# Attention softmax: context scores copied out of PSUM by VectorE with scale and minimum, one maximum per head, small two-input work moved to GpSimd

## The chip, the cores and the metric

The kernel runs on one core of a Trainium2 chip. A core has five engines with a queue each: TensorE (matmul; PE in the profile, its weight loads PEld), VectorE (DVE), ScalarE (ACT), GpSimd (POOL) and SyncE (SP, which issues DMAs here). An engine takes its instructions in the order of its queue, so an instruction that waits holds up all behind it. TensorE's results land in PSUM, which VectorE and ScalarE read; everything else lies in SBUF. The metric is device time in microseconds of one execution; the smaller the better.

## The reference

One layer of a diffusion backbone over 1024 latent tokens of width 1024, with 256 context tokens. After a modulated projection there are two attention branches with 8 query heads and 2 kv heads each (so 4 query heads to a kv head), head size 64:

```
A (windowed): scores of 128 queries against their block, the one before and the one after
              (band |q - k| <= 128), and the 256 context keys;
              m = max(scores, sink);  e = exp(scores - m);  p = e / (sum(e) + exp(sink - m))
B (global):   q and k normalised (RMS); scores against all 1024 latent and 256 context keys;
              p = softmax(scores)
o = p @ v     in each branch
y = (sigmoid(g_a) * (o_a @ w_a) + sigmoid(g_b) * (o_b @ w_b)) @ w_out
x = LN(alpha * x + gate * y), then a convolutional SwiGLU and a second LN
```

In both branches latent and context keys share one softmax. Everything is float32.

## The kernel before

The projections come first (to about 345 us of the profile), then attention, the merge with the branch matrices and `w_out`, and the feed-forward part from there to the end. float32 products are made of three or two products of float32r pieces: a tensor is split into a high part (a cast) and a low part (the difference).

Attention works in 32 units, `Unit(br, i, g)`: branch, block of 128 queries, kv group. The 16 units of branch A come first, then the 16 of B. A unit has two halves. The score half does, per head `h`, `lat(h)`: matmuls into a PSUM tile `s` (two buffers of 128x1024), a VectorE instruction which copies the scores out to `p`, multiplied by the negated scale, with the running minimum written to `nm` (so `nm` is minus the maximum), and ScalarE's `soft`, the exponential with its row sum in `sm`. `norm` then makes the reciprocal of the sum. The value half (`value_steps`) comes one unit later: `tr_step` transposes 128 keys of all four heads on TensorE into a PSUM tile (three buffers), ScalarE casts the high part `pth`, VectorE makes the low part `ptl` (for a few steps ScalarE copies out `prw` and GpSimd makes both); `av_step` multiplies them with the values into `av`; `out_step` copies `av` out as `avs`, adds its two halves (high and low part of the values) into `ot`, multiplies by the reciprocal sums `rb` and splits into `O`. `up` moves the second half to the first 64 partitions for that addition. `rows` turns the reciprocals `sm` into rows (a transposition `str`, a copy, a DMA to DRAM and two DMAs back that spread them over the partitions) for `rb`.

Branch A takes the scores of window and context together: a head's 640 columns (512 at the edges) are one `p` tile, and `norm` adds the exponential of the sink. Branch B has 1024 latent columns a head; its 256 context columns of all four heads stand in one tile, made ahead of the latent ones by `cxp`, and normalised by a maximum of their own: `reduce_max` (L470), a product with the scale (L471), and four exponentials straight from PSUM. The latent copies start from that maximum (`self.other`, `scalar2` of L458), so `nm` covers both, and `norm` brings the context side to it: a factor `f` (L482, L483), four products on GpSimd over the context probabilities (L486), and two small operations that join the sums (L487, L488). In branch A, `f` is the sink's term (L490 to L492).

The Python loop at L832 interleaves the two halves of consecutive units and, from unit 18 on, steps of the first branch matrix (`b`, `bT`, its weights split by GpSimd as `hwb`, `lwb`). The order in which the instructions finally stand on each engine is set by the build's scheduler, from priorities and its own estimate of times; so a small change of the source can move instructions of its neighbours too. GpSimd's queue also carries DMA issues (`sd`, L600) and the split of the queries (`qs`, in `qprep`, two units ahead).

Of the kernel before, what the change touches and what calls it, by code (L numbers as in the profile page):

```python
# [10 lines left out]
ALU = mybir.AluOpType  # L11
# [10 lines left out]
FF = 2816  # L22
NF = FF // P
GRID = 64
LN_EPS = 1e-5
QK_EPS = 1e-6
ALPHA = 2.0 ** 0.25
# [39 lines left out]
def layer_kernel(  # L67
# [315 lines left out]
    class Unit:  # L383
# [43 lines left out]
        def lat(self, h):  # L427
            kh = self.br * 2 + self.g
            s = None if self.w == 256 and h in S1 else s_tile(f"s{self.id}_{h}")
            if s is None:  # L430
                s = pt_tile(f"s{self.id}_{h}")
                self.qk(s[:, 0:256], h, KL[kh][:, self.k0:self.k0 + 256], False)
                if self.i == 0:
                    nc.tensor.matmul(s[:, 128:256], identr, maskr[:, 1], start=False, stop=True)
                else:
                    nc.tensor.matmul(s[:, 0:128], identr, maskr[:, 0], start=False, stop=True)
                self.qk(s[:, 256:512], h, KC[0][:, kh])
                o = s
            elif self.br == 1:
                for c in (0, 512):  # L440
                    self.qk(s[:, c:c + 512], h, KL[kh][:, c:c + 512])
                o = s
            else:
                w = self.w
                l = s[:, 512 - w:512]
                self.qk(l, h, KL[kh][:, self.k0:self.k0 + w], False)
                if w == 384:
                    nc.tensor.matmul(l.rearrange("p (a b) -> p a b", b=P)[:, 0::2, :], identr, maskr,
                                     start=False, stop=True)
                elif self.i == 0:  # L450
                    nc.tensor.matmul(l[:, 128:256], identr, maskr[:, 1], start=False, stop=True)
                else:
                    nc.tensor.matmul(l[:, 0:128], identr, maskr[:, 0], start=False, stop=True)
                self.qk(s[:, 512:512 + NC], h, KC[0][:, kh])
                o = s[:, 512 - w:512 + NC]
            hs = slice(h, h + 1)
            p = p_tile(f"p{self.id}_{h}")[:, 0:T if self.br else self.w + NC]
            nc.vector.tensor_scalar(out=p, in0=o, scalar1=self.qscale(nqs)[:, hs] if self.br else -1.0,  # L458
                                    scalar2=self.other[:, hs], op0=ALU.mult, op1=ALU.min, accum_out=self.nm[:, hs])
            self.soft(p, p, h, self.nm, self.sm, -1.0)  # L460
            self.pc[h, 0] = p

        def cxp(self):
            kh = self.br * 2 + self.g
            s = s_tile(f"s{self.id}_x")
            for h in range(4):
                self.qk(s[:, h * NC:(h + 1) * NC], h, KC[0][:, kh])
            self.other = small(f"nmc_{self.id}", (P, 4))
            self.smc = small(f"smc_{self.id}", (P, 4))
            nc.vector.reduce_max(self.other, s.rearrange("p (a b) -> p a b", a=4), axis=AX.X)  # L470
            nc.vector.tensor_tensor(out=self.other, in0=self.other, in1=self.qscale(nqs), op=ALU.mult)  # L471
            p = p_tile(f"p{self.id}_x")
            for h in range(4):
                self.pc[h, 1] = p[:, h * NC:(h + 1) * NC]
                self.soft(s[:, h * NC:(h + 1) * NC], self.pc[h, 1], h, self.other, self.smc,
                          self.qscale(pqs)[:, h:h + 1])

        def norm(self):
            hc = slice(self.g * 4, self.g * 4 + 4)
            f = small(f"f_{self.id}", (P, 4))  # L480
            if self.br:
                nc.vector.tensor_tensor(out=f, in0=self.nm, in1=self.other, op=ALU.subtract)  # L482
                nc.scalar.activation(f, f, AF.Exp)  # L483
                for h in range(4):
                    p = self.pc[h, 1]
                    nc.gpsimd.tensor_scalar(out=p, in0=p, scalar1=f[:, h:h + 1], scalar2=0.0, op0=ALU.mult, op1=ALU.add)  # L486
                nc.vector.tensor_tensor(out=self.smc, in0=self.smc, in1=f, op=ALU.mult)  # L487
                nc.vector.tensor_tensor(out=self.sm, in0=self.sm, in1=self.smc, op=ALU.add)  # L488
            else:
                nc.vector.tensor_tensor(out=f, in0=self.nm, in1=sinkb[:, hc], op=ALU.add)  # L490
                nc.scalar.activation(f, f, AF.Exp)
                nc.vector.tensor_tensor(out=self.sm, in0=self.sm, in1=f, op=ALU.add)  # L492
            nc.vector.reciprocal(self.sm, self.sm)

        def rows(self):
# [26 lines left out]
        def value_steps(self):  # L522
            nm, kt = self.id, self.kt
            vh = self.br * 2 + self.g
            parts = {}

            def tr_step(n):
                tr = pt_tile(f"ptr{nm}_{n}")
                for h in range(4):
                    nc.tensor.transpose(tr[:, h * P:(h + 1) * P], self.pslice(h, n), ident)  # L530
                hi = att.tile([P, 512], R32, tag="pth", name=f"pth{nm}_{n}", bufs=4)
                lo = att.tile([P, 512], R32, tag="ptl", name=f"ptl{nm}_{n}", bufs=4)
                pooled = n in POOL_LO[self.br]
                if pooled:
                    rw = att.tile([P, 512], F32, tag="ptr", name=f"prw{nm}_{n}", bufs=2)
                    nc.scalar.copy(rw, tr)  # L536
                    split(rw, hi, lo, nc.gpsimd, nc.gpsimd)
                else:
                    nc.scalar.copy(hi, tr)  # L539
                    nc.vector.tensor_tensor(out=lo, in0=tr, in1=hi.bitcast(F32), op=ALU.subtract)  # L540
                parts[n] = hi, lo
                return pooled

            def av_step(n):
                first = self.left == len(kt)
                self.left -= 1
                if first:
                    self.av = ps2.tile([P, 512], F32, tag="av", name=f"av{nm}")
                hi, lo = parts.pop(n)
                v = VT[kt[n] // 2][:, kt[n] % 2, vh]  # L550
                nc.tensor.matmul(self.av, v, hi, start=first, stop=False)  # L551
                nc.tensor.matmul(self.av, v, lo, start=False, stop=self.left == 0)  # L552

            def out_step():
                av = self.av
                avs = att.tile([P, 512], F32, tag="ptr", name=f"avs{nm}", bufs=2)
                nc.scalar.copy(avs, av)  # L557
                up = att.tile([HD, 512], F32, tag="up", name=f"up{nm}", bufs=1)
                nc.gpsimd.tensor_scalar(out=up, in0=avs[HD:P], scalar1=1.0, scalar2=0.0, op0=ALU.mult, op1=ALU.add)
                ot = att.tile([P, 2, P], F32, tag="ot", name=f"ot{nm}", bufs=1)  # L560
                for h in range(2):
                    nc.vector.tensor_tensor(out=ot[h * HD:(h + 1) * HD],
                                            in0=avs[0:HD].rearrange("p (a b q) -> p a b q", b=2, q=P)[:, :, h],
                                            in1=up.rearrange("p (a b q) -> p a b q", b=2, q=P)[:, :, h], op=ALU.add)
                nc.gpsimd.tensor_tensor(out=ot, in0=ot, in1=self.rb, op=ALU.mult)
                hf = self.i // 4
                qs = slice((self.i % 4) * P, (self.i % 4 + 1) * P)
                split(ot, otile(self.br, hf, 0, self.g)[:, :, qs], otile(self.br, hf, 1, self.g)[:, :, qs],
                      nc.gpsimd, nc.gpsimd)

            def step(ns):
                pooled = [tr_step(n) for n in ns]
                for n, pl in zip(ns, pooled):
                    clk[0] += 1
                    avq.append((self, n, clk[0] + LAG[self.br] + (PLAG[self.br] if pl else 0)))
                    av_issue()

            self.left = len(kt)
            self.av_step, self.out_step = av_step, out_step
            g = 1 + self.br  # L580
            steps = [lambda n=n: step(range(n, n + g)) for n in range(0, len(kt), g)]
            steps.insert(2 - self.br, self.rows)
            return steps

    tokens = []
# [184 lines left out]
    def small(name, shape):  # L770
        return att.tile(list(shape), F32, tag=name.split("_")[0], name=name,
                        bufs=4)
# [977 lines left out]
```

## Time and profile before

| what | value |
|---|---|
| time, median of 3 runs | 1577.16 us (1576.5 to 1577.59) |
| the profiled execution | 1580.51 us, span 1578.6 us, TensorE clock 0.994 |
| busy: PE, PEld, DVE, ACT, POOL | 1528.4, 1264.6, 1198.0, 808.9, 756.5 us |
| reciprocals of branch A (first, last) | 353.29, 475.50 us |
| reciprocals of branch B (first, last) | 489.43, 763.38 us |

A row of a timeline has the start and the length in us, engine, line, operation, output<-inputs, shapes, a count, and in brackets the idle time of the engine just before it and what ended it. When several equal instructions are merged, the length is that of all. A group has the count, the busy time, the mean of one in ns, and the idle time before them with what ended it. A stretch has its length, then busy time and count of PE, PEld, DVE, ACT and POOL, the clock, the DMA share and the DMA rate. A line of waits has the waiting instruction, the one waited for, us in total, times, and the longest. Line numbers are those of the kernel before, unless a row is of another kernel.

### The profile page before, as it was taken

How to read it: one execution, taken by the hardware profiler on the slowest of the kernel's cores; microseconds unless marked ns; L12 is line 12 of the kernel's file. 1: busy time of each engine (PE TensorE's matmuls, PEld its weight loads, DVE VectorE, ACT ScalarE, POOL GpSimd, SP SyncE). 2: the span in 40 equal slices, each digit the busy share in tenths (PEclk: the TensorE clock that was granted, in tenths of full speed). 3: DMA queues.
4: the chain of work that ended last, by engine and by line, in shares of the span. 5: the costliest groups of instructions: out<-in, count | busy, mean ns of one | idle time of the engine just before them, and what ended most of it. 6: DMA issues, size and time to landing. Idle time of an engine off the chain costs nothing.

```text
span 1578.6 us, 21930 instructions
## 1 busy us (share of the span) xinstructions
PE 1528.4 (97%) x7614; PEld 1264.6 (80%) x7614; DVE 1198.0 (76%) x1761; ACT 808.9 (51%) x1439; POOL 756.5 (48%) x737
## 2 busy tenths in 40 slices
PE   6999999999999999999999999999999999999997
PEld 5878788878886887777788898888888888888886
DVE  7797645628888777788675679888888888656797
ACT  5422222448888667688522466444444444435533
POOL 0573312426666566655432544666667765021053
PEclk9999999999999999999999999999999999999999
DMA  9685662322227555532344132333334446996723
GB/s 378 218 313 187 213 219 87 120 79 74 64 82 180 138 128 127 128 84 41 130 160 93 54 107 81 121 107 107 107 107 107 107 111 178 364 270 221 244 92 107
DMA packets 112015, 230.25 MB, mean 146 GB/s; under 512 B 13504, under 2 KB 27328, under 8 KB 111808
## 3 DMA queue, kind: packets, MB, share of 16 engines
q1 hardware_dynamic: 96464, 199.20, 37.9%
q0 software_dynamic: 10400, 20.19, 8.2%
q10 hardware_dynamic: 5040, 9.46, 1.6%
q8 instruction: 60, 0.98, 0.3%
q14 instruction: 51, 0.42, 0.1%
HBM read 177.61 MB, written 65.87 MB: 154 GB/s over the span
## 4 chain that ended last, share of the span: by engine, by line
PE 73%; DVE 12%; DMA 5%; ACT 4%; issue 3%; POOL 1%; SPq 0%; ACTq 0%; DVEq 0%; POOLq 0%
PE ptr L530 5%; PE b L91 3%; PE b L90 3%; PE b L89 3%; PE g L89 3%; PE g L91 3%; PE g L90 3%; PE s L413 2%; PE av L551 2%; PE c L90 2%; PE d L90 2%; PE a L90 2%; PE c L89 2%; PE d L89 2%; PE a L89 2%
## 5 line engine op out<-in xcount | busy, mean ns | idle before, releaser
L540 DVE TENSOR_TENSOR ptl<-ptr,pth 128x512 fp32r<-128x512 f32 x188 | 124.6, 684 | 27.8 <-ACT pth L539 25.6
L86 DVE TENSOR_TENSOR ld<-rd,hd 128x1024 fp32r<-128x1024 f32 x77 | 97.6, 1284 | 50.8 <-ACT hd L81 48.7
L530 PE MATMUL ptr<-ident,p 128*128 128x128 f32 x816 | 126.7, 278 | 9.2 <-DVE ptl L540 6.8
L539 ACT CAST pth<-ptr 128x512 fp32r<-128x512 f32 x188 | 106.5, 588 | 56.5 <-PE ptr L530 32.8
L425 ACT ACTIVATE p<-p,nm 128x1024 f32<-128x1024 f32 (+2 forms) x128 | 125.3, 981 | 11.1 <-DVE p L458 10.3
L530 PEld LDWEIGHTS ptr<-ident,p 128*128 128x128 f32 x816 | 93.6, 140 | 39.6 <-DVE ptl L540 13.9
L81 ACT CAST hd<-rd 128x1024 fp32r<-128x1024 f32 x77 | 79.4, 1050 | 88.5 <-PE p L91 60.4
L551 PE MATMUL av<-pth,VT 128*128 128x512 f32 x236 | 104.6, 443 | 1.0 <-ACT avs L557 0.5
L90 PE MATMUL p<-ld,hd 128*128 128x512 f32 x264 | 103.5, 392 | 0.3 <-DVE ld L86 0.3
L89 PE MATMUL p<-hd 128*128 128x512 f32 x264 | 103.8, 393 | 0.0
L91 PE MATMUL p<-hd,ld 128*128 128x512 f32 x264 | 103.5, 392 | 0.0
L89 PE MATMUL g<-hh,whg 128*128 128x512 f32 x256 | 99.9, 390 | 0.0
L91 PE MATMUL g<-hh,wlg 128*128 128x512 f32 x256 | 99.7, 389 | 0.0
L90 PE MATMUL g<-hl,whg 128*128 128x512 f32 x256 | 99.6, 389 | 0.0
L552 PE MATMUL av<-ptl,VT 128*128 128x512 f32 x236 | 97.7, 414 | 1.9 <-POOL ptl L86 1.8
L86 POOL TENSOR_TENSOR wlg<-wg,whg 128x512 fp32r<-128x512 f32 x32 | 44.2, 1388 | 112.7 <-ACT whg L81 109.2
L458 DVE TENSOR_SCALAR_CACHE_REDUCE p<-s,cvt,nmc 128x1024 f32<-128x1024 f32 x64 | 84.4, 1339 | 12.3 <-PE s L414 11.8
L413 PE MATMUL s<-KL,q 128*128 128x512 f32 (+2 forms) x192 | 76.0, 396 | 2.9 <-ACT p_x L425 2.0
L187 DVE CUSTOM_DVE_ANT_0 wml<-wml,sc,bmc 128x1024 f32<-128x1024 f32 x32 | 45.6, 1435 | 40.6 <-DMA wml<-in_wmodT_dram 39.7
L83 POOL TENSOR_SCALAR pth<-prw 128x512 fp32r<-128x512 f32 x48 | 31.0, 646 | 87.8 <-ACT prw L536 62.3
L414 PE MATMUL s<-KL,q 128*128 128x512 f32 (+2 forms) x192 | 71.7, 373 | 0.0
L81 ACT CAST wS<-s 128x512 fp32r<-128x512 f32 x76 | 45.3, 621 | 51.0 <-POOL s L1083 50.2
(402 smaller groups left out, 4945.7 us busy)
## 6 DMA issues: line engine op xcount, KB each, us to landing
wml<-in_wmodT_dram SPq DMA_DIRECT2D x48, 512.0 KB
ru<-in_w_up_dram SPq DMA_DIRECT2D x38, 512.0 KB
rd<-td SPq DMA_DIRECT2D x55, 256.0 KB
rd<-sd SPq DMA_DIRECT2D x44, 256.0 KB
rd<-in_w_dn_dram SPq DMA_DIRECT2D x33, 256.0 KB
wm<-in_wmodT_dram SPq DMA_DIRECT2D x16, 512.0 KB
wg<-in_w_g_dram SPq DMA_DIRECT2D x32, 256.0 KB
sgd<-sg ACTq DMA_DIRECT2D x32, 256.0 KB
```

Source lines behind the costliest of these rows:

```text
L81: cast[:] = [nc.scalar.copy(hi, src).ins]
L86: low[:] = [lo_eng.tensor_tensor(out=lo, in0=src, in1=hi.bitcast(F32), op=ALU.subtract).ins]
L89: nc.tensor.matmul(ps, a[0], b[0], start=start, stop=False, skip_group_check=resumed)
L90: nc.tensor.matmul(ps, a[0], b[1], start=False, stop=False, skip_group_check=resumed)
L91: nc.tensor.matmul(ps, a[1], b[0], start=False, stop=stop, skip_group_check=resumed)
L413: nc.tensor.matmul(o, self.q[0][:, hs], ks, start=True, stop=False)
L425: nc.scalar.activation(p, s, AF.Exp, bias=nm[:, h:h + 1], scale=scale, accum_out=sm[:, h:h + 1])
L530: nc.tensor.transpose(tr[:, h * P:(h + 1) * P], self.pslice(h, n), ident)
L539: nc.scalar.copy(hi, tr)
L540: nc.vector.tensor_tensor(out=lo, in0=tr, in1=hi.bitcast(F32), op=ALU.subtract)
L551: nc.tensor.matmul(self.av, v, hi, start=first, stop=False)
L552: nc.tensor.matmul(self.av, v, lo, start=False, stop=self.left == 0)
```

## The change

In branch B `cxp` no longer takes a maximum of the context scores. For each head it copies the 256 context scores out of PSUM to `p`, scaled and negated, with their minimum written to `other`; the latent copy starts from it as before. The exponentials of the context columns come after those of the latent ones of the same head, from SBUF and with the head's one maximum `nm`, so that the factor `f`, the four products on GpSimd and the joining of unequal sums go away; what is left is one addition of two sums. Small additions with two SBUF inputs (`sm` of both branches, `f` of branch A, and the two halves of `ot`) are issued on GpSimd in place of VectorE. `rows` stands one step later among the value steps: in branch A after three transposition steps in place of two, in B after the second pair in place of the first.

```diff
+TOP = 3.0e38
...
             self.soft(p, p, h, self.nm, self.sm, -1.0)
             self.pc[h, 0] = p
+            if self.br:
+                self.soft(self.pc[h, 1], self.pc[h, 1], h, self.nm, self.smc, -1.0)
 
         def cxp(self):
...
-            nc.vector.reduce_max(self.other, s.rearrange("p (a b) -> p a b", a=4), axis=AX.X)
-            nc.vector.tensor_tensor(out=self.other, in0=self.other, in1=self.qscale(nqs), op=ALU.mult)
             p = p_tile(f"p{self.id}_x")
             for h in range(4):
-                self.pc[h, 1] = p[:, h * NC:(h + 1) * NC]
-                self.soft(s[:, h * NC:(h + 1) * NC], self.pc[h, 1], h, self.other, self.smc,
-                          self.qscale(pqs)[:, h:h + 1])
+                c = slice(h * NC, (h + 1) * NC)
+                self.pc[h, 1] = p[:, c]
+                nc.vector.tensor_scalar(out=p[:, c], in0=s[:, c], scalar1=self.qscale(nqs)[:, h:h + 1], scalar2=TOP,
+                                        op0=ALU.mult, op1=ALU.min, accum_out=self.other[:, h:h + 1])
 
         def norm(self):
             hc = slice(self.g * 4, self.g * 4 + 4)
-            f = small(f"f_{self.id}", (P, 4))
-            if self.br:
-                nc.vector.tensor_tensor(out=f, in0=self.nm, in1=self.other, op=ALU.subtract)
-                nc.scalar.activation(f, f, AF.Exp)
-                for h in range(4):
-                    p = self.pc[h, 1]
-                    nc.gpsimd.tensor_scalar(out=p, in0=p, scalar1=f[:, h:h + 1], scalar2=0.0, op0=ALU.mult, op1=ALU.add)
-                nc.vector.tensor_tensor(out=self.smc, in0=self.smc, in1=f, op=ALU.mult)
-                nc.vector.tensor_tensor(out=self.sm, in0=self.sm, in1=self.smc, op=ALU.add)
-            else:
-                nc.vector.tensor_tensor(out=f, in0=self.nm, in1=sinkb[:, hc], op=ALU.add)
-                nc.scalar.activation(f, f, AF.Exp)
-                nc.vector.tensor_tensor(out=self.sm, in0=self.sm, in1=f, op=ALU.add)
+            more = self.smc if self.br else small(f"f_{self.id}", (P, 4))
+            if not self.br:
+                nc.gpsimd.tensor_tensor(out=more, in0=self.nm, in1=sinkb[:, hc], op=ALU.add)
+                nc.scalar.activation(more, more, AF.Exp)
+            nc.gpsimd.tensor_tensor(out=self.sm, in0=self.sm, in1=more, op=ALU.add)
             nc.vector.reciprocal(self.sm, self.sm)
...
                 for h in range(2):
-                    nc.vector.tensor_tensor(out=ot[h * HD:(h + 1) * HD],
+                    nc.gpsimd.tensor_tensor(out=ot[h * HD:(h + 1) * HD],
                                             in0=avs[0:HD].rearrange("p (a b q) -> p a b q", b=2, q=P)[:, :, h],
                                             in1=up.rearrange("p (a b q) -> p a b q", b=2, q=P)[:, :, h], op=ALU.add)
...
             steps = [lambda n=n: step(range(n, n + g)) for n in range(0, len(kt), g)]
-            steps.insert(2 - self.br, self.rows)
+            steps.insert(3 - self.br, self.rows)
             return steps
```

## The prediction

> **What bounds the kernel now.** I read the page's engine totals first, then busy time by stretch for the two attention stages, and then the timeline of single engines inside one unit of branch A. A unit is one (branch, query block, kv group); A is the windowed branch (`br` 0), B the global one (`br` 1).
>
> ```profile
> PE 1528.4 (97%) x7614; PEld 1264.6 (80%) x7614; DVE 1198.0 (76%) x1761; ACT 808.9 (51%) x1439; POOL 756.5 (48%) x737
> 383.40:458.90 75.50, 75.14 (x497) 63.64 (x496) 65.47 (x154) 64.79 (x154) 48.93 (x73) 1.00 0.25 67
> 505.80:763.40 257.60, 248.33 (x1415) 201.59 (x1415) 202.83 (x350) 188.23 (x417) 149.88 (x206) 1.00 0.45 104
> ```
>
> TensorE looks full (its ends are modelled), so idle time has to be looked for in the order of the queues. The two stretches run from the first to the last of ten reciprocals of A, and over nearly all of B. In A VectorE (third figure) and ScalarE (fourth) are at 87% and 86%, GpSimd at 65%; in B VectorE is at 79%.
>
> ```profile
> 383.41 0.18 DVE L493 RECIPROCAL sm<-sm 128x4 f32<-128x4 f32 x1
> 458.88 0.18 DVE L493 RECIPROCAL sm<-sm 128x4 f32<-128x4 f32 x1
> ...
> 424.68 0.48 DVE L492 TENSOR_TENSOR sm<-sm,f 128x4 f32<-128x4 f32 x1 [1.02 <-ACT f L491]
> 425.19 0.18 DVE L493 RECIPROCAL sm<-sm 128x4 f32<-128x4 f32 x1
> 425.28 0.85 DVE L458 TENSOR_SCALAR_CACHE_REDUCE p<-s,negsink 128x640 f32<-128x640 f32 x1
> 426.06 1.88 DVE L540 TENSOR_TENSOR ptl<-ptr,pth 128x512 fp32r<-128x512 f32 x3
> 427.86 0.87 DVE L458 TENSOR_SCALAR_CACHE_REDUCE p<-s,negsink 128x640 f32<-128x640 f32 x1
> 428.66 0.88 DVE L458 TENSOR_SCALAR_CACHE_REDUCE p<-s,negsink 128x640 f32<-128x640 f32 x1
> 431.17 0.93 DVE L562 TENSOR_TENSOR ot<-avs,up 64x256 f32<-64x256 f32 x2
> 432.13 0.16 DVE L490 TENSOR_TENSOR f<-nm,sinkb 128x4 f32<-128x4 f32 x1
> ```
>
> One reciprocal ends each unit. From 383.41 to 458.88 there are nine steps: 75.47 / 9 = 8.39 us per unit. In the unit shown VectorE runs nearly without a gap; its one steady wait is 1.02 us before `sm`, for ScalarE's exponential of the sink. So VectorE's queue closes the loop in A. Two starts in a row give the pitch of an instruction: a score copy 0.80, a `ptl` 0.60 (1.80 for three), a reciprocal 0.09.
>
> **The change in stage A.** VectorE loses two `ot` additions, `f` and `sm`. The additions go to GpSimd's queue, and what matters is where they stand. In the built program GpSimd's order for one inner A unit (here 0_3_0 to 0_3_1) is:
>
> ```
> sm 3_0 | qs 5_0 (cast) | up 2_1 | qs 5_0 (low part) | ot 2_1 x2 | ot*rb 2_1 | O cast | O low | f 3_1 | pth 3_0 | ptl 3_0 | sm 3_1
> VectorE: reciprocal 3_0 | ptl | ptl | score copy 3_1, head 0 | ptl | copy | copy | ptl | copy | reciprocal 3_1 ...
> ScalarE: f 3_0 | pth x4 | exp 3_1, head 0 | avs 2_1 | exp | exp | rb | q | prw | exp | f 3_1 ...
> ```
>
> VectorE's reciprocal now waits for GpSimd's `sm`; behind it in VectorE's queue stand the next unit's `ptl` and score copies, for which TensorE, and through ScalarE's first exponential `avs`, wait; and GpSimd's `up` waits for that `avs`. This is a closed loop through three engines, and all of GpSimd's output work lies on it. Its prices:
>
> ```profile
> 423.82 0.62 POOL L83 TENSOR_SCALAR pth<-prw 128x512 fp32r<-128x512 f32 x1 [1.06 <-DMA rb<-dn]
> 424.40 0.73 POOL L565 TENSOR_TENSOR ot<-ot,rb 128x256 f32<-128x256 f32 x1
> 425.10 1.28 POOL L86 TENSOR_TENSOR ptl<-prw,pth 128x512 fp32r<-128x512 f32 x1
> 426.35 0.40 POOL L83 TENSOR_SCALAR O<-ot 128x256 fp32r<-128x256 f32 x1
> 426.83 0.73 POOL L86 TENSOR_TENSOR O<-ot,O 128x256 fp32r<-128x256 f32 x1
> 429.46 0.41 POOL L83 TENSOR_SCALAR qs<-Q 128x256 fp32r<-128x256 f32 x1 [1.90 <-PE qtr L403]
> 429.95 0.61 POOL L559 TENSOR_SCALAR up<-avs 64x512 f32<-64x512 f32 x1
> 430.65 0.74 POOL L86 TENSOR_TENSOR qs<-Q,qs 128x256 fp32r<-128x256 f32 x1
> ...
> 429.19 0.59 ACT L557 COPY avs<-av 128x512 f32<-128x512 f32 x1
> 429.66 0.84 ACT L425 ACTIVATE p<-p,nm 128x640 f32<-128x640 f32 x1
> 430.49 0.83 ACT L425 ACTIVATE p<-p,nm 128x640 f32<-128x640 f32 x1
> ...
> 429.37 0.42 PE L413 MATMUL s<-KL,q 128*128 128x384 f32 x1
> 430.04 0.28 PE L414 MATMUL s<-KC,q 128*128 128x256 f32 x1
> ...
> L321 POOL TENSOR_SCALAR cvt<-cvt 128x8 f32<-128x8 f32 x8 | 2.5, 307 | 0.7
> ```
>
> From one reciprocal to the next:
> - Reciprocal to the end of the next head-0 copy: 0.09 + 2 x 0.60 + 0.80 = 2.1 us. Then either exponential and `avs` on ScalarE (pitch 0.83, copy 0.59: 3.5 us), or, in every second unit, where `av`'s last product is queued on TensorE behind a score group waiting for that copy's buffer, 0.8 us of the group, its product and the copy, some 3.9. `qs` before `up` waits for a transposition behind the same group, to about 4.0. I take 3.9 to the start of `up`. In the trace `up` starts 4.76 us after the reciprocal (425.19 to 429.95), with one `ptl` more ahead of it, so 3.9 is no pessimism.
> - `up` 0.70, `qs` 0.74, two `ot`, `ot*rb` 0.73, `O` 0.48 and 0.74. The 64x256 addition is not in the trace on GpSimd; a 64x512 `up` costs what a 128x512 `pth` does, so its price goes by the free size: the 128x256 addition at 0.73 is nearest. Bounds: 0.40 (the one-input `O` cast) and 0.93 (VectorE's pair as one). With 1.46 for two the piece is 4.85.
> - `f`, `pth` 0.58, `ptl` 1.25, `sm`. Of a 128x4 addition on GpSimd the nearest row is 128x8 with one input, 0.31; bounds 0.16 (VectorE's `f`) and 0.40. 2.45, and 0.1 for hand-overs.
>
> Sum 3.9 + 4.85 + 2.45 + 0.1 = 11.3 us against 8.39, so +2.9 on nine inner steps: +26 us. With both low prices the loop is 10.3 (+17), with both high ones 11.9 (+31). GpSimd's pitches alone add up to some 8.0, so it is not full: it stands idle in front of `avs`. ScalarE's exponential of the sink waits for GpSimd's `f`, hidden behind GpSimd's own `pth` and `ptl`. Around the nine: between the sums of 0_1_1 and 0_2_0 GpSimd has two output steps in a row; these and the first and last units add 0 to 6, I take +3. `rows` one step later (its transposition, the `rb` copy, three DMA issues on SP) costs nothing: `ot*rb` now comes one loop and 6.8 us behind its reciprocal, where before GpSimd's `pth` even waited for that landing (423.82). If that cover went, GpSimd would wait 1 us a unit.
>
> **The change in stage B.** Here the score copies of the context replace a maximum and a product, and the head's one maximum removes `f`, `smc` and four scalings.
>
> ```profile
> L458 DVE TENSOR_SCALAR_CACHE_REDUCE p<-s,cvt,nmc 128x1024 f32<-128x1024 f32 x56 | 73.9, 1339 | 10.6 <-PE s L414 10.1
> L562 DVE TENSOR_TENSOR ot<-avs,up 64x256 f32<-64x256 f32 x28 | 18.5, 662 | 6.6 <-POOL up L559 6.4
> L470 DVE TENSOR_REDUCE nmc<-s_x 128x4 f32<-128x1024 f32 x13 | 15.8, 1214 | 1.6 <-PE s_x L414 1.6
> L482 DVE TENSOR_TENSOR f<-nm,nmc 128x4 f32<-128x4 f32 x14 | 5.9, 424 | 0.1
> L488 DVE TENSOR_TENSOR sm<-sm,smc 128x4 f32<-128x4 f32 x14 | 4.8, 346 | 0.1
> L471 DVE TENSOR_TENSOR nmc<-nmc,cvt 128x4 f32<-128x4 f32 x13 | 4.5, 349 | 0.2
> L487 DVE TENSOR_TENSOR smc<-smc,f 128x4 f32<-128x4 f32 x14 | 2.9, 204 | 2.6 <-ACT f L483 2.5
> ...
> L486 POOL TENSOR_SCALAR p_x<-p_x,f 128x256 f32<-128x256 f32 x64 | 29.8, 496 | 10.6 <-ACT f L483 10.6
> ...
> PEld ptr L530 <- DVE ptl L540: 11.8, 24, 1.5
> PEld s L413 <- ACT p_x L425: 3.4, 5, 1.1
> ...
> L458 DVE TENSOR_SCALAR_CACHE_REDUCE p<-s,negsink 128x640 f32<-128x640 f32 x36 | 30.8, 873 | 0.2 <-PE s L414 0.2
> L492 DVE TENSOR_TENSOR sm<-sm,f 128x4 f32<-128x4 f32 x9 | 4.3, 478 | 9.1 <-ACT f L491 9.1
> ```
>
> Per unit VectorE loses 1.21 + 0.42 + 0.35 + 0.35 + 0.20 + 2 x 0.66 = 3.9 us. It gains four copies of 128x256: from 1.339 at 1024 and 0.873 at 640, 1.2 ns an element, so 0.41 each, 1.6 in all. Net -2.2. GpSimd loses 4 x 0.50 and gains 1.46 + 0.31: level. ScalarE loses only `f`. In B this is off TensorE's path except where TensorE waits: for `ptl` 11.8 us and for the context exponentials, which held the score buffer, 3.4 us; 15.2 in all. I take 11 of it as gained, bounds 0 and 18. The new wait: the reciprocal needs `sm` from GpSimd, behind two exponentials on ScalarE after the last score copy; VectorE has some 2.5 us of `ptl` and next-unit copies queued ahead, so I take 2 us in all, bounds 0 and 1.28 a unit (one `ptl` of GpSimd ahead of `sm`). Net -9.
>
> **Sum.** +26 + 3 - 9 = +20. The profiled execution took 1580.5 us (span 1578.6), 3.3 above the median of 1577.2; the difference is put on the median: 1597 us. With the bounds of A's prices and of B's gain, the case's own range is 1584 to 1612.
>
> [...] VectorE's `sm` of 128x4 takes 0.478 where `f`, the same shape, takes 0.16; at 424.68 it lasted until 425.16, and GpSimd's `ot*rb` from 424.40 until 425.13. [...]
>
> **Rivals.**
> - *GpSimd runs ahead, faster.* If `up` did not have to wait for the next unit's `avs`, GpSimd would be held only by its own 8.0 us per unit, under 8.39. [...] For it: GpSimd is idle for a third of A. Against it: the order above puts `sm`, reciprocal, copy and `avs` in a ring. It decides if `up` starts within 1.0 us of the reciprocal.
> - *VectorE bounds B, faster.* If the 2.2 us were all on the path, B gains 35; with A's low price (+17 + 3) the time is 1562 too. Against it: VectorE waits for ScalarE and TensorE in B (10.1 for `s` alone). It decides from a gain in B of over 20.
> - *B's reciprocals queue behind GpSimd as well, slower.* `sm` stands there behind `qs`, a DMA issue or a weight split; with that 1.28 us on each of 16 units, +20: 1617.
> - *No change.* A's loss at its low end, +20 with the edges, against a B gain of 20.
>
> **Chances.** A's ring 0.70 (1597); B's reciprocals too 0.10 (1617); the two faster cases 0.17 (1562); even 0.03. Faster by over 0.2% 0.17, within 0.2% (some 3 us, about what a measurement of this kernel can tell from no change) 0.03, slower 0.80. The range reaches from 1572 to 1614.
>
> **What would show it.** In the profile after: reciprocals of A 11 us apart; VectorE idle 2 us or more before each, released by GpSimd's `sm`; ScalarE's `f` waiting for GpSimd; GpSimd idle before `up`; no VectorE `sm` or `ot`. In B: TensorE's waits for `ptl` down to a few us, none for `p_x`. The forecast is wrong if A's reciprocals stay 8.4 us apart, or if B shortens by more than 20 us.

## The result and the profile after

The changed kernel takes 1619.76 us (median, 1618.36 to 1621.66) against 1577.11 before: ratio 1.0271, 95% interval 1.0254 to 1.0289. The profiled execution has a span of 1618.8 us, 40.2 more than the one before. It was forecast slower, at 1597; it is slower by twice as much.

The page of the changed kernel, its engine totals and the clock row of its 40 slices (one slice is 40.5 us):

```profile
PE 1541.6 (95%) x7614; PEld 1284.2 (79%) x7614; DVE 1141.3 (70%) x1713; ACT 802.9 (50%) x1423; POOL 784.8 (48%) x785
PEclk9999999999888999999999999999999999999999
```

Busy time by stretch: nine inner steps of branch A (before: 75.50 us, clock 1.00), and branch B from its first to its last reciprocal:

```profile
388.10:505.30 117.20, 89.82 (x492) 77.86 (x492) 53.44 (x118) 65.12 (x152) 64.78 (x108) 0.84 0.16 40
537.90:806.80 268.90, 262.58 (x1505) 215.75 (x1504) 187.66 (x383) 196.40 (x433) 162.54 (x214) 0.99 0.49 114
```

A step of A takes 117.2 / 9 = 13.02 us in place of 8.39, and every engine has idle time in it. The granted clock, 1.00 there before, is 0.84; in the page it is the three 8s of the clock row. Branch B went from 273.95 us (489.43 to 763.38) to 268.93.

VectorE's reciprocals at both ends of one loop of A, ScalarE's `avs` and its exponential of the sink between them, TensorE's transposition `qtr`, and GpSimd's part of the loop:

```profile
426.83 0.18 DVE L487 RECIPROCAL sm<-sm 128x4 f32<-128x4 f32 x1 [5.64 <-POOL sm L486]
440.33 0.18 DVE L487 RECIPROCAL sm<-sm 128x4 f32<-128x4 f32 x1 [5.33 <-POOL sm L486]
...
430.60 0.57 ACT L551 COPY avs<-av 128x512 f32<-128x512 f32 x1
...
431.62 0.81 PE L404 MATMUL qtr<-identr,qs 128*128 128x128 f32 x4
...
438.25 0.21 ACT L485 ACTIVATE f<-f 128x4 f32<-128x4 f32 x1 [2.25 <-POOL f L484]
...
432.53 0.40 POOL L84 TENSOR_SCALAR qs<-Q 128x256 fp32r<-128x256 f32 x1 [5.73 <-PE qtr L404]
433.01 0.61 POOL L553 TENSOR_SCALAR up<-avs 64x512 f32<-64x512 f32 x1
433.71 0.73 POOL L87 TENSOR_TENSOR qs<-Q,qs 128x256 fp32r<-128x256 f32 x1
434.40 1.53 POOL L556 TENSOR_TENSOR ot<-avs,up 64x256 f32<-64x256 f32 x2
436.01 0.74 POOL L559 TENSOR_TENSOR ot<-ot,rb 128x256 f32<-128x256 f32 x1
...
438.02 0.20 POOL L484 TENSOR_TENSOR f<-nm,sinkb 128x4 f32<-128x4 f32 x1
...
440.10 0.20 POOL L486 TENSOR_TENSOR sm<-sm,f 128x4 f32<-128x4 f32 x1
```

This is the ring of the prediction: the reciprocal is held by GpSimd's `sm`, ScalarE's `f` waits for GpSimd, GpSimd stands idle (5.73 us here) ahead of its output work. One link is another than the prediction named. `up` is not held by `avs`, which is done at 431.17; it stands in GpSimd's queue behind the cast of `qs`, and that waits for TensorE's `qtr`, until 432.53. So it is in all of the nine loops: `up` starts 0.48 to 0.49 us behind the start of that cast in eight of them, 0.62 in the ninth, with `avs` done before. From the start of `up` to the reciprocal it is 440.33 - 433.01 = 7.32 us, where the prediction has 4.85 + 2.45 + 0.1 = 7.40. What is longer is the other half: from the reciprocal to `up` 433.01 - 426.83 = 6.18 us, where the prediction has 3.9 (over the nine steps 5.13 to 6.19, mean 5.71). TensorE shows why, in its rows just behind the first reciprocal:

```profile
424.62 0.28 PE L415 MATMUL s<-KC,q 128*128 128x256 f32 x1
427.66 1.11 PE L524 MATMUL ptr<-ident,p 128*128 128x128 f32 x4 [2.75 <-DVE ptl L534]
428.42 0.77 PE L545 MATMUL av<-pth,VT 128*128 128x512 f32 x1
429.00 0.63 PE L546 MATMUL av<-ptl,VT 128*128 128x512 f32 x1
429.42 0.63 PE L545 MATMUL av<-pth,VT 128*128 128x512 f32 x1
429.85 0.63 PE L546 MATMUL av<-ptl,VT 128*128 128x512 f32 x1
```

After 2.75 us of idle time four transpositions take 428.42 - 427.66 = 0.76 us, and products with 512 columns follow each other by 0.42 us. In the rows ahead of the idle time the pitch of 512 columns is 0.23 (420.33 to 420.56), and the granted clock is 0.50 from 426.86 to 433.69. So the ring makes TensorE idle, and behind that idle time TensorE is slow here (clock 0.50) in the very work, up to `qtr`, that GpSimd's `qs` and `up` wait for.

Against the kernel before, the 40.2 us of the span are: first reciprocal of A 2.5 later, A 169.89 in place of 122.21 (+47.7), from A to B 12.14 in place of 13.93 (-1.8), B -5.0, the rest behind it -3.2.

### The profile page after: what moved, and what is told of

It is laid out like the page before. It is cut to its first block, busy times and chain, and to the rows that moved or that the text cites. A ratio compares the mean times of both kernels' runs of the same rounds, so it can differ in the third digit from the quotient of the medians.

```text
span 1618.8 us, 21977 instructions
## 1 busy us (share of the span) xinstructions
PE 1541.6 (95%) x7614; PEld 1284.2 (79%) x7614; DVE 1141.3 (70%) x1713; ACT 802.9 (50%) x1423; POOL 784.8 (48%) x785
## 4 chain that ended last, share of the span: by engine, by line
PE 79%; POOL 7%; DMA 4%; DVE 3%; issue 3%; ACT 2%; SPq 0%; DVEq 0%; ACTq 0%; POOLq 0%
PE ptr L524 5%; PE p L91 3%; PE p L90 3%; PE p L92 3%; PE b L92 3%; PE av L545 3%; PE b L91 3%; PE b L90 3%; PE g L90 3%; PE g L91 3%; PE g L92 3%; PE av L546 3%; PE c L91 2%; PE a L91 2%; PE d L91 2%
## 5 line engine op out<-in xcount | busy, mean ns | idle before, releaser
L524 PEld LDWEIGHTS ptr<-ident,p 128*128 128x128 f32 x816 | 98.7, 144 | 50.6 <-DVE ptl L534 27.2
L545 PE MATMUL av<-pth,VT 128*128 128x512 f32 x236 | 109.5, 464 | 3.6 <-POOL pth L84 2.7
L546 PE MATMUL av<-ptl,VT 128*128 128x512 f32 x236 | 101.7, 431 | 3.2 <-POOL ptl L87 3.2
L414 PE MATMUL s<-KL,q 128*128 128x512 f32 (+2 forms) x192 | 79.3, 413 | 10.6 <-DVE p L459 6.7
L415 PE MATMUL s<-KL,q 128*128 128x512 f32 (+2 forms) x192 | 73.8, 384 | 0.1
L82 ACT CAST wA<-ru 128x512 fp32r<-128x512 f32 x57 | 35.5, 623 | 60.5 <-PE d L92 32.4
```

The costliest lines, as they stand in the source:

```text
L82: cast[:] = [nc.scalar.copy(hi, src).ins]
```

## The experiments

In all of them the ratio is that to the kernel before on the same chip. The steps are the nine inner ones of A.

### Which branch: A's moves alone, and all but A's moves

The kernel before, with A's share of the moves:

```diff
-                nc.vector.tensor_tensor(out=f, in0=self.nm, in1=sinkb[:, hc], op=ALU.add)
+                nc.gpsimd.tensor_tensor(out=f, in0=self.nm, in1=sinkb[:, hc], op=ALU.add)
...
-                nc.vector.tensor_tensor(out=self.sm, in0=self.sm, in1=f, op=ALU.add)
+                nc.gpsimd.tensor_tensor(out=self.sm, in0=self.sm, in1=f, op=ALU.add)
...
-                    nc.vector.tensor_tensor(out=ot[h * HD:(h + 1) * HD],
+                    (nc.vector if self.br else nc.gpsimd).tensor_tensor(out=ot[h * HD:(h + 1) * HD],
...
-            steps.insert(2 - self.br, self.rows)
+            steps.insert(1 if self.br else 3, self.rows)
```

> The kernel before, with branch A's moves alone: A's f, sm and the two ot additions on GpSimd, A's rows one step later; branch B's code as before. Theory (the whole loss is A's ring through GpSimd; B's part of the change is a gain of about 10): reciprocals of A about 13 us apart in the inner steps, sum over A +50, time 1577 + 50 = 1627, at least 1618. Rival 1 (a good part of the loss is made in B or at the changeover, where the copies and their waits are new): A's part alone costs less, about +30 to +40, 1607 to 1617. Rival 2 (A is only slow because what B does in its first units reaches back into it): 1577 to 1585.

The changed kernel, with A as it was:

```diff
-                nc.gpsimd.tensor_tensor(out=more, in0=self.nm, in1=sinkb[:, hc], op=ALU.add)
+                nc.vector.tensor_tensor(out=more, in0=self.nm, in1=sinkb[:, hc], op=ALU.add)
...
-            nc.gpsimd.tensor_tensor(out=self.sm, in0=self.sm, in1=more, op=ALU.add)
+            (nc.gpsimd if self.br else nc.vector).tensor_tensor(out=self.sm, in0=self.sm, in1=more, op=ALU.add)
...
-                    nc.gpsimd.tensor_tensor(out=ot[h * HD:(h + 1) * HD],
+                    (nc.gpsimd if self.br else nc.vector).tensor_tensor(out=ot[h * HD:(h + 1) * HD],
...
-            steps.insert(3 - self.br, self.rows)
+            steps.insert(2, self.rows)
```

> The changed kernel, with branch A as in the kernel before: its f, sm and ot on VectorE, its rows after two steps; B as changed. Theory: A back at 8.4 us per reciprocal with TensorE's granted clock at 1.0, B's gain of about 10 stays: 1577 - 10 = 1567 (1564 to 1571), faster than the kernel before. Rival (the gain seen in B and behind it is only what a late end of A leaves to it, work that waited in A and was then done at once): 1574 to 1580, no gain.

A's moves alone take 1629.64 us (ratio 1.033, 1.0302 to 1.0359), with steps of 12.67 us. All but A's moves take 1566.51 us (0.9936, 0.9919 to 0.9953), with steps of 8.39 us; this kernel is faster than both. The stretch of the nine steps, first of A's moves alone:

```profile
387.36:501.35 113.99, 85.34 (x492) 72.62 (x492) 53.25 (x117) 64.59 (x152) 64.99 (x108) 0.89 0.16 41
```

and of the kernel with A as before:

```profile
382.50:458.10 75.60, 75.23 (x498) 63.68 (x496) 65.56 (x154) 64.92 (x154) 49.15 (x73) 1.00 0.25 67
```

A's moves cost 1629.64 - 1577.45 = 52 us and the rest gives 1577.45 - 1566.51 = 11; together +41, and the whole change measured +43. The two add up; nothing of the loss is made in B.

### Opening the ring, and shortening it

With A's two sums on VectorE, so that no GpSimd instruction stands ahead of A's reciprocal:

```diff
-                nc.gpsimd.tensor_tensor(out=more, in0=self.nm, in1=sinkb[:, hc], op=ALU.add)
+                nc.vector.tensor_tensor(out=more, in0=self.nm, in1=sinkb[:, hc], op=ALU.add)
...
-            nc.gpsimd.tensor_tensor(out=self.sm, in0=self.sm, in1=more, op=ALU.add)
+            (nc.gpsimd if self.br else nc.vector).tensor_tensor(out=self.sm, in0=self.sm, in1=more, op=ALU.add)
```

> The changed kernel, with A's f and sm alone back on VectorE; all ot additions stay on GpSimd, rows stays later. This opens the ring at its last link (GpSimd's sum to VectorE's reciprocal) and leaves GpSimd's load but for 0.4 us per unit. Theory (the ring costs, not the load): inner steps of A 8.2 to 8.8 us apart, clock 1.0 in A, time 1563 to 1575. Rival 1 (GpSimd's load of the ot additions costs, 1.6 us of pitch per unit, since up, qs and O stand in one queue with pth and ptl that TensorE needs): inner steps 10 us or more, time 1590 or more. Rival 2 (half of it: the low-part ptl and pth of GpSimd come late, the ring being only one of two): inner steps 9 to 10, 1575 to 1590.

With both branches' `ot` additions on VectorE, the sums left on GpSimd:

```diff
-                    nc.gpsimd.tensor_tensor(out=ot[h * HD:(h + 1) * HD],
+                    nc.vector.tensor_tensor(out=ot[h * HD:(h + 1) * HD],
```

> The changed kernel, with the ot additions of both branches back on VectorE; f and sm stay on GpSimd, so the link from GpSimd's sum to VectorE's reciprocal stays. Theory: the ring stays closed but is shorter; GpSimd's two additions (1.6 us of pitch) become VectorE's pair (0.9 us, with one hand-over each way), and what waits before up stays: inner steps of A between 9.5 and 12.3 us, time 1585 to 1610; if with it the idle gaps of TensorE fall under about 2 us and the clock stays at 1.0, near the low end. Rival (GpSimd's load alone costs): with the load gone, inner steps at 8.4, time 1567 to 1577.

The open ring takes 1585.03 us (1.0044, 1.0027 to 1.0061), steps of 9.65 us; the shorter one 1585.26 (1.0049, 1.0034 to 1.0064), steps of 9.47 us. The open ring did not go as my theory had it (8.2 to 8.8) but as its second rival: there is a second ring. Rows of TensorE, GpSimd and VectorE of the kernel with A's sums on VectorE:

```profile
424.98 0.50 PE L546 MATMUL av<-ptl,VT 128*128 128x512 f32 x1 [0.85 <-POOL ptl L87]
...
427.15 0.41 POOL L84 TENSOR_SCALAR qs<-Q 128x256 fp32r<-128x256 f32 x1 [2.21 <-PE qtr L404]
...
431.01 0.39 DVE L486 TENSOR_TENSOR sm<-sm,f 128x4 f32<-128x4 f32 x1 [1.91 <-ACT f L485]
```

GpSimd also makes `pth` and `ptl` of one key tile per unit, behind its output work; TensorE's `av` product waits for that `ptl`, and behind it in TensorE's queue stand the scores, the product that ends `av`, and the transposition `qtr`, for which GpSimd's `qs` and the output work behind it wait. Both waits stand in each of the nine steps: TensorE waits for `ptl` 7.1 us in all, GpSimd for `qtr` 18.6. `ot` on GpSimd lengthens this ring by its pitch, 1.6 us; that is read from the order of the queues, and no run opened this second ring by itself. The table of steps of A then reads: neither move 8.39, `ot` alone 9.65 (+1.3), sums alone 9.47 (+1.1), both 13.02 (+4.6). Together they cost 2.3 us more than the two apiece. All but the first of the four have `rows` one step later in A, which was not run there by itself.

The kernel with `ot` on VectorE has the first ring still closed, its reciprocal waiting for GpSimd, but the waits of TensorE behind it are short and the clock stays up (a row each of VectorE and TensorE, and the stretch of its nine steps):

```profile
434.13 0.18 DVE L487 RECIPROCAL sm<-sm 128x4 f32<-128x4 f32 x1 [2.33 <-POOL sm L486]
434.95 0.66 PE L524 MATMUL ptr<-ident,p 128*128 128x128 f32 x4 [0.95 <-DVE ptl L534]
...
387.24:472.50 85.26, 73.97 (x485) 63.35 (x483) 63.22 (x132) 64.26 (x152) 53.22 (x89) 1.00 0.21 55
```

### Is it the clock? The same order, with shorter instructions in the ring

Three kernels in which GpSimd's two-input instructions of branch A are replaced, one for one, by copies with one input. On TensorE, VectorE and ScalarE the order of the instructions in the nine steps is that of the changed kernel. A copy leaves out what its instruction computed: in the first kernel the low part of one key tile per unit, in the second the low part of A's output as well, in the third also the half of the sum `ot` that comes from `avs`. The `one` argument of `split` is new:

```diff
+        if one:
+            lo_eng.tensor_scalar(out=lo, in0=src, scalar1=1.0, scalar2=0.0, op0=ALU.mult, op1=ALU.add)
+            return
...
-                    split(rw, hi, lo, nc.gpsimd, nc.gpsimd)
+                    split(rw, hi, lo, nc.gpsimd, nc.gpsimd, not self.br)
```

> The changed kernel, with GpSimd's ptl in branch A (the low part of the one key tile per unit that GpSimd splits) as a copy with one input in place of a subtraction with two; so that tile's low part is wrong in the output, on all else the order on every engine is the same. GpSimd's pth, a copy of the same size, has a pitch of 0.58 where ptl has 1.25: the ring is 0.67 us shorter. Theory L (the step is a plain sum; TensorE's low granted clock is a by-product): inner steps of A 13.02 - 0.67 = 12.35 us, clock in A as low as before (0.84), time about 1619.8 - 13 x 0.67 = 1611. Theory C (the extra over the forecast is the clock: after some 3 us idle TensorE runs at half rate, which delays av, avs and up): either as L, if the idle time of TensorE is still long enough for it, or, if it falls under that length, the clock goes to 1.0 and the step falls by some 1.6 us more, to 10.7.

The second has this too, in `out_step`:

```diff
-                      nc.gpsimd, nc.gpsimd)
+                      nc.gpsimd, nc.gpsimd, not self.br)
```

> As the run before, and the low part of branch A's O on GpSimd also a copy with one input (pitch 0.49 in place of 0.74 to 0.80; A's output loses its low part): the ring is about 0.95 us shorter in all, the order of the engines the same. Theory L: steps of 13.02 - 0.95 = 12.1, clock about 0.85, time about 1607. Theory C: 12.1 if the idle time still suffices, 10.4 to 10.6 with clock 1.0 if not; time then about 1590.

and the third this:

```diff
                 for h in range(2):
+                    if not self.br:
+                        nc.gpsimd.tensor_scalar(out=ot[h * HD:(h + 1) * HD],
+                                                in0=up.rearrange("p (a b q) -> p a b q", b=2, q=P)[:, :, h],
+                                                scalar1=1.0, scalar2=0.0, op0=ALU.mult, op1=ALU.add)
+                        continue
```

> As the run before, and the two ot additions of branch A on GpSimd also copies with one input (of up alone, so A's output is wrong): nearest row is the O cast, 0.40 to 0.49, so some 0.35 us each less; the ring is about 1.65 us shorter in all, the order of the engines the same. Theory L: steps of 11.4, clock below 1.0 in A, time about 1598. Theory C: TensorE's idle time (2.9 to 3.5 us with the whole ring) falls to some 1.5 to 2 us, the clock in A is 1.0, the pitch of 512-column matmuls is 0.23 in all of it, the time from the reciprocal to up is about 4.2 as where ot stood on VectorE, steps 9.6 to 9.9, time 1577 to 1585. It is this run which the two tell apart most: 11.4 or 9.8.

The three took 1603.19 us (1.0162, 1.0147 to 1.0177), 1598.38 (1.0129, 1.0108 to 1.0151) and 1586.82 (1.0057, 1.0042 to 1.0072). The stretch of their nine steps, in a fence each:

```profile
382.16:488.35 106.19, 85.53 (x492) 73.47 (x492) 53.06 (x118) 65.16 (x153) 58.85 (x108) 0.89 0.17 44
```

```profile
382.56:479.36 96.80, 78.88 (x492) 66.53 (x492) 52.21 (x118) 64.77 (x153) 55.68 (x108) 0.96 0.19 49
```

```profile
383.94:472.59 88.65, 76.41 (x492) 63.78 (x492) 52.07 (x117) 64.59 (x153) 49.90 (x108) 1.00 0.21 54
```

| kernel | step | `up` to reciprocal | reciprocal to `up`, each of the nine | clock |
|---|---|---|---|---|
| changed | 13.02 | 7.32 | 5.13 to 6.19 | 0.84 |
| first | 11.80 | 6.57 | two of 4.2 and 4.4; seven of 5.1 to 5.9 | 0.89 |
| second | 10.76 | 6.14 | seven of 4.2 to 4.4; 5.27 and 5.67 | 0.96 |
| third | 9.85 | 5.51 | all 4.18 to 4.42 | 1.00 |

GpSimd's half became 7.32 - 5.51 = 1.81 us shorter, the step 13.02 - 9.85 = 3.17 us: 1.36 us more than was taken away. That is the other half, which no edit touched: 5.71 us on average at a clock of 0.84, 4.35 at 1.00. A plain sum (theory L) expected steps of 12.35, 12.1 and 11.4; theory C named 10.7 or 12.35, 10.5 or 12.1, and 9.6 to 9.9. The last and most telling came out at 9.85. In the first two, loops of both kinds stand beside each other. The time of the third kernel is 2 us over what C expected (1577 to 1585).

The run with A's moves alone shows the same within one program. There the unit of the loop shown above happened to run at full clock. TensorE's rows and GpSimd's `up` behind the reciprocal at 426.29 (line numbers of the kernel before):

```profile
427.12 0.66 PE L530 MATMUL ptr<-ident,p 128*128 128x128 f32 x4 [3.22 <-DVE ptl L540]
427.53 0.48 PE L551 MATMUL av<-pth,VT 128*128 128x512 f32 x1
427.85 0.40 PE L552 MATMUL av<-ptl,VT 128*128 128x512 f32 x1
428.09 0.40 PE L551 MATMUL av<-pth,VT 128*128 128x512 f32 x1
...
430.47 0.62 POOL L559 TENSOR_SCALAR up<-avs 64x512 f32<-64x512 f32 x1
```

The idle time ahead is longer than in the changed kernel's loop (3.22 against 2.75), yet the products follow each other by 0.24 us in place of 0.42, and `up` starts 430.47 - 426.29 = 4.18 us after the reciprocal in place of 6.18. The same work at the same place of the order costs 2.0 us less at full clock. Of the nine loops of this run one more has 4.18 us, and the other seven, at half clock for a part, have 5.47 to 5.92.

### Branch B: copies, GpSimd's small work, and the place of `rows`

Four kernels take B's gain of 11 us apart. In the kernel with A as before, B's sum and `ot` went back to VectorE:

```diff
-            (nc.gpsimd if self.br else nc.vector).tensor_tensor(out=self.sm, in0=self.sm, in1=more, op=ALU.add)
+            nc.vector.tensor_tensor(out=self.sm, in0=self.sm, in1=more, op=ALU.add)
...
-                    (nc.gpsimd if self.br else nc.vector).tensor_tensor(out=ot[h * HD:(h + 1) * HD],
+                    nc.vector.tensor_tensor(out=ot[h * HD:(h + 1) * HD],
```

> The kernel before with the copies and the one maximum of branch B alone: all sums and ot of both branches on VectorE, A's rows as before (B's rows one step later). Theory (B's gain is the saved work on VectorE and on ScalarE's and GpSimd's side of the factor f, the small moves to GpSimd in B add the rest): VectorE has 2 x 0.66 + 0.2 us per unit more than in the kernel with A as before, so the gain of 11 shrinks: 1566.5 + 2 to 8 = 1568 to 1575. Rival (the moves in B only add a wait before the reciprocal and the copies give all of the gain): 1560 to 1566.

or the sum alone (the first of the two edits):

> The kernel with A as before and B as changed (1566.5 us), with B's one sum also back on VectorE; B's ot stays on GpSimd. Theory (GpSimd's sum makes the reciprocal wait 8.8 us in the whole of B, nearly all of it beside TensorE's work): no more than 3 us either way, 1563 to 1569. Rival (those waits are on the path): 1566.5 - 6 to 9 = 1558 to 1561.

or B's `rows` went back to its old place, everything else as in the kernel with A as before:

```diff
-            steps.insert(2, self.rows)
+            steps.insert(2 - self.br, self.rows)
```

> The kernel with A as before and B as changed (1566.5 us), with B's rows after the first pair of key tiles, as in the kernel before. Prediction's reading (rows later costs nothing and hides the landing of rb): within 3 us of 1566.5. Rival (the later rows is needed, since GpSimd's sum now makes the reciprocal late and TensorE's transposition of it would wait in its place): TensorE waits up to 1 to 2 us in each of 16 units, 1575 to 1590.

The same edit on top of the one with all sums and `ot` on VectorE:

> The kernel before with B's copies and one maximum, all sums and ot on VectorE and B's rows as before. With the rows later this took 1573.1 (1568.6 to 1577.0; the profiled one, of span 1568.8, some 1570.7). Theory (the copies give the gain in B; the place of rows matters only with the sum on GpSimd): 1568 to 1577. Rival (the place of rows gives the gain whichever engine makes the sum): 1577 to 1585.

and its reverse on the kernel before:

> The kernel before, with B's rows after the second pair of key tiles in place of the first, and nothing else. Theory (rows later only helps where GpSimd's sum makes the reciprocal late; in the kernel before no reciprocal of B waits for GpSimd): 1574 to 1580, no change. Rival (all of B's gain of about 11 comes from the later rows, the copies giving nothing): 1564 to 1569.

| B's code | `rows` at its old place | `rows` later |
|---|---|---|
| as before | 1 (1577) | 0.9996, 0.9987 to 1.0005 (1577.86) |
| copies, small work on VectorE | 0.9985, 0.9973 to 0.9997 (1576.61) | 0.9968, 0.9954 to 0.9982 (1573.07) |
| copies, sum on VectorE, `ot` on GpSimd | not run | 0.9944, 0.9923 to 0.9964 (1568.03) |
| copies, sum and `ot` on GpSimd | 1.0023, 1.0012 to 1.0034 (1581.67) | 0.9936, 0.9919 to 0.9953 (1566.51) |

The copies with one maximum give 2 to 5 us by themselves. With `rows` later, `ot` on GpSimd gives some 4 to 5 more (the intervals 0.9954 to 0.9982 and 0.9923 to 0.9964 still overlap), and the sum's engine makes no difference that these runs can tell, as expected of it. With `rows` at its old place the moves to GpSimd turn a gain into a loss of 4 us: 14 to 15 us for one step of the list, where I expected no more than 3. The rows of GpSimd, VectorE and TensorE in the fourth unit of B, with `rows` at its old place:

```profile
540.37 1.20 POOL L87 TENSOR_TENSOR O<-ot,O 128x256 fp32r<-128x256 f32 x1
...
544.13 0.43 POOL L486 TENSOR_TENSOR sm<-sm,smc 128x4 f32<-128x4 f32 x1
544.60 0.18 DVE L487 RECIPROCAL sm<-sm 128x4 f32<-128x4 f32 x1 [4.32 <-POOL sm L486]
...
545.21 0.80 PE L414 MATMUL s<-KL,q 128*128 128x512 f32 x1 [3.97 <-DVE p_x L477]
```

and with `rows` later:

```profile
541.41 0.42 POOL L486 TENSOR_TENSOR sm<-sm,smc 128x4 f32<-128x4 f32 x1
541.87 0.18 DVE L487 RECIPROCAL sm<-sm 128x4 f32<-128x4 f32 x1 [1.29 <-POOL sm L486]
...
542.48 0.50 PE L414 MATMUL s<-KL,q 128*128 128x512 f32 x1 [0.94 <-DVE p_x L477]
```

With `rows` early the scheduler also puts the unit's output work on GpSimd early, ahead of `sm`; the reciprocal then waits 4.32 us, the last context copy `p_x` stands behind it on VectorE, and TensorE waits 3.97 us for that copy's buffer. This is the ring of A in B, at one place. TensorE's other waits between 486 and 765 us of that kernel are up to 1.77 us each; how the rest of the 14 to 15 us divides among them was not taken apart, nor was why `rows` later helps a little (3 us, intervals that overlap) with everything on VectorE. One thing that the place of `rows` does, with the copies, shows in the waits of TensorE's weight loads for `ptl`, over the whole of B. With `rows` early, small work on GpSimd and then on VectorE:

```profile
PEld ptr L524 <- DVE ptl L534: 10.5, 20, 2.0
PEld ptr L524 <- DVE ptl L534: 10.1, 21, 1.7
```

and with `rows` later, in the same order:

```profile
PEld ptr L524 <- DVE ptl L534: 4.1, 11, 0.9
PEld ptr L524 <- DVE ptl L534: 2.6, 11, 0.5
```

In the kernel before they are 12.4 us, and with `rows` later but without the copies still 9.2: it takes both.

## Why the prediction was wrong in size

- **The mechanism in A: right but for one link.** The ring through VectorE's reciprocal, TensorE and GpSimd's output work was there, with the waits that were forecast. It comes back to GpSimd by `qtr` and the cast of `qs`, though, and not by ScalarE's `avs`. Taking A's moves out removes the loss (8.39 us a step), and with them alone the loss is there (12.67).
- **"I take 3.9 to the start of `up`": the step that failed.** It measures 5.71, and two terms are missing. The smaller one is the cast of `qs`, 0.49 us of GpSimd's queue between `qtr` and `up`. The prediction lets `qs` wait "to about 4.0" and yet starts `up` at 3.9, and its list of GpSimd's work has only the low part of `qs`; the cast is put at nothing. At full clock the cast starts 3.86 us after the reciprocal and `up` 4.35 (means of the third shortened kernel). The prediction's own rows have it, `qs` at 429.46 and `up` at 429.95, and the 4.76 us that it read there is the longest of the nine steps; the other eight are 4.48 to 4.50. The larger term is the 1.36 us of TensorE at half rate after its idle time: in the changed kernel the cast starts at 5.20. The prediction forecast VectorE's idle time ("VectorE idle 2 us or more before each"), from which TensorE's follows, and priced what came behind it by rows of a kernel whose TensorE had hardly stood still there (busy 75.14 of 75.50 us). On nine steps: +26 forecast, +12 for the clock, +4 for the cast, -1 for GpSimd's half, 41 in all; measured 117.2 - 75.5 = 41.7.
- **GpSimd's prices: right.** The two `ot` additions took 1.53 (forecast 1.46, bounds 0.80 to 1.86), `f` and `sm` 0.20 each (0.31, bounds 0.16 to 0.40).
- **The edges of A, +3: too small.** A as a whole grew by 47.7 us, so 6.0 lie outside the nine steps.
- **`rows` one step later costs nothing: right for B, but it has a worth there that was put at nothing.** By itself it changes nothing (0.9996). With the copies and the moves to GpSimd it decides between a gain of 11 us and a loss of 4: GpSimd's output work comes behind `sm`, and the waits for `ptl` go. In A it was not run by itself.
- **B at -9: right in size, in part by luck.** A as before with B changed is 11 us faster, and the waits of TensorE's weight loads in B went as forecast: for `ptl` from 11.8 to 2.9 us, and none for ScalarE's `p_x` (3.4 before). The second is the work of the copies; it is gone with `rows` at either place. The first was put down to VectorE's lighter load, but with that load and the early `rows` it stays at 10.1 and 10.5 us, as shown above. The moves to GpSimd were counted in that load (2 x 0.66 us) and given no price of their own: with the copies and `rows` later alone `ptl` is down as well, but 5.0 us of waits for VectorE's score copies stand there (1.7 before), and half of the gain is gone. The waits in B, of the changed kernel:

```profile
PEld ptr L524 <- DVE ptl L534: 2.9, 10, 0.9
```

and of the kernel with the copies alone:

```profile
PEld s L414 <- DVE p L459: 5.0, 6, 1.3
PEld ptr L524 <- DVE ptl L534: 2.6, 11, 0.5
```

- **The rivals.** GpSimd did not run ahead (in the nine steps `up` starts 5.13 us or more after the reciprocal, not within 1.0). No run shows what makes up this rival's 1562; what the runs showed in its place is A 47.7 us longer and, with A as before, B's part 11 us faster by the copies, the moves and the later `rows`. B's reciprocals did not make B slower (B -5.0 us; eight of its sixteen reciprocals waited for GpSimd, one 6.14 us, the others 0.27 to 1.59). "VectorE bounds B" did not come either: the gain in B is 11 us, not 35.
- **The case's own range.** With the bounds that the prediction names (A's two prices, B's gain of 0 to 18, its new wait at 2) it is 1581 to 1613, not 1584 to 1612. The measured 1619.76 lies above either.

## What to carry to other kernels

When a small instruction moves to another engine's queue, follow both directions: what it waits for there, and which of that engine's own inputs come from the engine that now waits for it. If the two close a ring, the sum of the pitches along the ring is the step (here 7.32 + 5.71 for 13.02 us), with every instruction that stands in a queue between two of its links (here a cast of 0.49 us that has nothing to do with the output); and two moves that cost 1.1 and 1.3 us each cost 4.6 together. And when a forecast makes TensorE idle for 2 us or more per step (seven of nine loops were slow behind 2.06 to 2.58 us), do not price the work behind the gap by rows from a stretch without gaps: here it ran at half rate for a time, and that was 12 of the 42 us lost in the nine steps.

## What the runs showed of the hardware that was not expected

In these runs TensorE's half rate did not need a long stop, and no single length of it decided. Taking the idle time just ahead of TensorE's first work after A's reciprocal, as the profile gives it: none of nine loops was slow at 1.2 to 1.5 us (third shortened kernel), two of nine at 1.6 to 2.2 (second), seven of nine at 2.1 to 2.6 (first; TensorE busy for 0.39 to 0.50 of the 3.41 us ahead of the slow ones), all nine at 2.7 to 4.0 (changed kernel), but two loops stayed at full clock behind 3.22 and 2.98 us (A's moves alone). What goes with it shows in the granted clock, with time cut at 423.45, 426.86 and so on in steps of 3.41 us; from 388 to 506 us of the changed kernel the clock changes at such cuts alone (389.32, 392.73, 402.97, 406.38 and so on):

```profile
423.45:426.86 3.41, 1.46 (x12) 1.25 (x10) 0.03 (x1) 1.65 (x4) 3.18 (x6) 1.00 0.18 49
426.86:430.27 3.41, 2.61 (x8) 2.23 (x9) 3.41 (x7) 0.98 (x2) 0.00 (x0) 0.50 0.00 0
430.27:433.69 3.42, 3.42 (x16) 3.25 (x15) 1.63 (x5) 2.58 (x7) 1.02 (x2) 0.50 0.02 5
433.69:437.10 3.41, 3.41 (x25) 3.07 (x25) 0.89 (x2) 2.20 (x6) 3.15 (x5) 1.00 0.43 146
```

In the changed kernel the clock is 0.50 or 1.00 for whole stretches of this grid. It was at half in one or two in a row in each of the changed kernel's nine loops, and in seven, two and none of the nine in the three shortened kernels, just the loops with a late `up`. In the nine steps of these four kernels every full-clock stretch in which TensorE was busy for a share of 0.50 or less (here 1.46 of 3.41 us, 0.43) was followed by one at half clock, and every one with 0.51 or more by one at full clock (in the changed kernel alone 0.47 and less, and 0.57 and more). With A's moves alone the border is not as sharp: two with 0.47 and 0.49 were followed by full clock, one with 0.55 by half. So the half rate goes here with how much of one stretch an idle time empties, rather than with its length: a loop behind 3.22 us stayed at full clock, and seven of nine behind 2.06 to 2.58 us did not. That the 3.22 us fell across the border of two stretches is my reading; no figure here shows it.
